# Queries and keys projected feature-major and stacked by DMA, and a new order of units at the attention's end

## Chip, cores and metric

The kernel runs on one core of one Trainium2 chip. The metric is device time in microseconds (us) of that core, from one launch that does the whole step. Nothing else runs on the core.

## What is computed

One step of a two-layer network for 128 context tokens and 512 latent tokens. Each layer has three branches that read one input projection: a state-space mixer, differential attention, and a gated MLP. The change lies in the attention branch. Cut to that branch, the reference is:

```python
q = q.reshape(bt, T, DA_HEADS, 2, DA_QK)            # 8 heads, 2 maps, 64 wide
k = k.reshape(bt, T, DA_HEADS, 2, DA_QK)
v = v.reshape(bt, T, DA_HEADS, DA_VD)               # 128 wide
if latent:                                          # 512 tokens; context: 128, no rotary
    k_all = concatenate([ctx_k, apply_rope(k, cos, sin)], 1)   # 128 cached keys first
    v_all = concatenate([ctx_v, v], 1)
    q = apply_rope(q, cos, sin)
s = einsum("bqhmd,bkhmd->bhmqk", q, k_all) * DA_QK ** -0.5
p = softmax(s, axis=-1)
w = p[:, :, 0] - lam * p[:, :, 1]
o = rmsnorm(einsum("bhqk,bkhd->bqhd", w, v_all), head_norm_w) * (1 - lam_init)
y_b = o.reshape(bt, T, DA_INNER) * silu(g_b)
```

`apply_rope` takes the 64 numbers of a map as two halves of 32 and returns `[x1*c - x2*s, x1*s + x2*c]`. Everything is float32 in the interface. To keep that precision, the kernel splits an operand into a rounded high part (type fp32r) and a low part that holds the rest, and sums the products of the parts that matter.

## The kernel before, in words

The 640 tokens are five tiles of 128; tile 0 is the context. The work is a list of units (`schedule`). A unit is one slice of a weight matrix, and each is computed as three products of parts (high x high, high x low, low x high) over eight blocks of 128 features:

- T units (`dense_T`, L469 to L471) hold a token tile in the array and stream weights: the result has tokens on the partitions. For each tile there are 24 matmuls, as wide as the unit.
- F units (`dense_F`, L529 to L531) hold weights and stream tokens: the result has features on the partitions and tokens along the row. There are two halves of 320 tokens, 24 matmuls each.

Per layer the order is eight T units qkvg (one a head: q, k, v and gate, 512 columns), three T units sv of the MLP (352 columns), then pairs of F units mgb and brb that gate and project the attention's output, and then the other branches (u, gc, xbc, mgc, brc, z, mga, bra) and the output projection wo.

Around this stream of dense matmuls run tasks. A task is a generator; it yields a number of ticks until its next step. A tick passes after three or six dense matmuls (`tick`), and it is the only clock: what a task issues is put into the engines' queues at that place in the order. `force` runs ticks without matmuls until a condition holds. `w_advance` loads weights (512 KB a chunk, L383 on SyncE's queue), copies the high part on ScalarE (L405) and subtracts the low part on VectorE (L414); up to five chunks stand ready. The list is run once with a stand-in for the engines, a plan places all buffers, and then it is run again to write the instructions.

For each head and tile, `head_evac` takes the projection out of PSUM with tokens on partitions, rotates q and k there (L849, L852, L853, on VectorE), splits both (`split_k`, `split_q`), transposes four blocks that hold the stacked high and low parts (L870) and one with q's low part (L871), and copies them out of PSUM (L876, L880). `head_cache` does the same for the cached keys with two transposes (L895). `scores` is one task for each head and tile: for each map the stacked high part of q against the stacked parts of k (L917, 128 rows high), and the low part of q against the high part of k (L922, 64 rows high, the two maps on the two halves of the array); row maxima (L929), exponentials with sums (L935), the combined weights (L942), their transposes (L951), and the product with v (L968). It uses two pairs of PSUM banks, of the group "s". `head_y` normalises, gates and transposes the head's output; `split_b` splits the eight outputs for the brb units. Scores of head h run while head h+1 is projected (`before`), those of head 7 beside the first sv unit.

## Time and profile before

| | |
|---|---|
| median of 3 runs | 2299.95 us (2299.92 to 2301.16) |
| profiled execution | 2299.74 us, span 2298.0 us |
| TensorE busy | 2253.0 us, 98% |
| VectorE busy | 1416.6 us, 62% |
| ScalarE busy | 1018.7 us, 44% |
| DMA | 218.52 MB, mean 95 GB/s |
| granted TensorE clock | 0.994 of full speed |

The page gives the busy time of each engine, the span in 40 slices, the chain of work that ended last, and the costliest groups of instructions. The start and length of a matmul row in the timeline are not its price: matmuls overlap, so the price of one in a stream is the distance from its start to the next one's. The attention stages lie at about 60 to 450 us (layer 0) and 1170 to 1600 us (layer 1) of the span.

### The profile page before, as it was taken

Reading aid. Unit: us, or ns where it says so; the run is one execution under the profiler, and the core shown is the slowest. Engines: PE = TensorE matmul, PEld = TensorE weight load, DVE = VectorE, ACT = ScalarE, POOL = GpSimd, SP = SyncE. Lnnn points to the kernel's source line nnn. Section 1 sums busy time; section 2 is a strip of 40 time slices with the busy share of each in tenths; the row PEclk is TensorE's granted clock in tenths of the full one; section 3 lists DMA queues with packets and bytes.
Section 4 is the critical chain, followed back from the end, with each engine's and each line's share of the span. In section 5 each row is a group of like instructions: output and inputs, shape, how many; then the busy total and the mean of one; then the engine's idle time right before and its main releaser. Section 6 shows DMA issues by size and latency. Waiting matters only on the chain.

```text
span 2298.0 us, 37200 instructions
## 1 busy us (share of the span) xinstructions
PE 2253.0 (98%) x14618; PEld 2044.9 (89%) x14618; DVE 1416.6 (62%) x2918; ACT 1018.7 (44%) x2386; POOL 184.8 (8%) x196
## 2 busy tenths in 40 slices
PE   7999999999999999999989999999999999999998
PEld 4788888999999999998868888889999999999986
DVE  6777777652454258976377777776424432789754
ACT  4555555521333247662265555554223322677421
POOL 1000000000100112320000000000000101132100
PEclk9999999999999999999999999999999999999999
DMA  7121110333223235534231112102222231555351
GB/s 287 56 63 43 60 59 29 107 131 129 92 65 104 83 82 147 164 104 158 90 115 64 43 60 63 61 18 98 83 74 74 66 112 57 143 138 147 105 184 46
DMA packets 80551, 218.52 MB, mean 95 GB/s; under 512 B 10284, under 2 KB 23660, under 8 KB 80376
## 3 DMA queue, kind: packets, MB, share of 16 engines
q1 hardware_dynamic: 80376, 216.15, 29.3%
q8 instruction: 115, 1.88, 0.4%
q14 instruction: 60, 0.49, 0.1%
HBM read 206.37 MB, written 8.68 MB: 94 GB/s over the span
## 4 chain that ended last, share of the span: by engine, by line
PE 84%; DVE 7%; ACT 4%; issue 2%; DMA 2%; SPq 0%; POOL 0%; DVEq 0%; ACTq 0%; POOLq 0%
PE psum L529 14%; PE psum L530 14%; PE psum L531 14%; PE psum L469 10%; PE psum L470 9%; PE psum L471 8%; PE psum L968 3%; PE psum L917 2%; PE psum L951 2%; PE psum L922 2%; PE psum L666 1%; DVE rounded L414 1%; PE psum L870 1%; PE psum L1088 1%; DMA plain<-csd 1%
## 5 line engine op out<-in xcount | busy, mean ns | idle before, releaser
L530 PE MATMUL psum<-shared,rounded 128*128 128x320 f32 x2624 | 812.2, 310 | 5.8 <-DVE shared L1062 5.8
L529 PE MATMUL psum<-shared,rounded 128*128 128x320 f32 x2624 | 816.5, 311 | 0.0
L531 PE MATMUL psum<-shared,rounded 128*128 128x320 f32 x2624 | 810.5, 309 | 0.0
L529 PEld LDWEIGHTS psum<-shared,rounded 128*128 128x128 f32 x2624 | 497.2, 189 | 19.0 <-issue 14.3
L530 PEld LDWEIGHTS psum<-shared,rounded 128*128 128x128 f32 x2624 | 492.9, 188 | 8.3 <-DVE shared L1062 7.3
L531 PEld LDWEIGHTS psum<-shared,rounded 128*128 128x128 f32 x2624 | 493.2, 188 | 0.0
L414 DVE TENSOR_TENSOR rounded<-plain,rounded 128x1024 fp32r<-128x1024 f32 (+2 forms) x214 | 266.0, 1244 | 250.0 <-ACT rounded L405 240.1
L469 PE MATMUL psum<-rounded,shared 128*128 128x512 f32 (+1 forms) x900 | 362.0, 402 | 2.1 <-DVE plain L1034 2.1
L470 PE MATMUL psum<-rounded,shared 128*128 128x512 f32 (+1 forms) x900 | 339.8, 378 | 0.0
L471 PE MATMUL psum<-rounded,shared 128*128 128x512 f32 (+1 forms) x900 | 338.7, 376 | 0.9 <-DVE shared L796 0.9
L405 ACT CAST rounded<-plain 128x1024 fp32r<-128x1024 f32 (+2 forms) x214 | 222.8, 1043 | 212.4 <-PE psum L530 194.1
L469 PEld LDWEIGHTS psum<-rounded,shared 128*128 128x128 f32 x900 | 170.0, 189 | 35.4 <-issue 10.3
L471 PEld LDWEIGHTS psum<-rounded,shared 128*128 128x128 f32 x900 | 169.8, 189 | 31.0 <-DVE shared L796 1.2
L470 PEld LDWEIGHTS psum<-rounded,shared 128*128 128x128 f32 x900 | 170.6, 190 | 20.8 <-DVE rounded L414 0.5
L1600 ACT ACTIVATE plain<-psum 128x320 f32<-128x320 f32 x96 | 41.6, 436 | 205.8 <-PE psum L531 198.4
L929 DVE TENSOR_REDUCE plain<-psum 128x1 f32<-128x640 f32 (+1 forms) x160 | 107.1, 711 | 35.8 <-PE psum L922 35.8
L935 ACT ACTIVATE plain<-psum,plain 128x640 f32<-128x640 f32 (+1 forms) x160 | 111.0, 699 | 21.0 <-DVE plain L929 17.4
L876 DVE CAST shared<-psum 128x512 fp32r<-128x512 f32 x64 | 44.2, 691 | 99.6 <-PE psum L870 99.4
L968 PEld LDWEIGHTS psum<-plain 128*128 128x128 f32 x640 | 81.0, 191 | 4.7
L974 ACT ACTIVATE plain<-psum,plain 128x128 f32<-128x128 f32 x80 | 29.4, 368 | 119.0 <-PE psum L968 103.2
L968 PE MATMUL psum<-plain 128*128 128x128 f32 x640 | 81.7, 275 | 0.0
L1028 ACT ACTIVATE plain<-psum 128x320 f32<-128x320 f32 (+1 forms) x62 | 27.8, 448 | 106.1 <-PE psum L531 69.4
(321 smaller groups left out, 3017.6 us busy)
## 6 DMA issues: line engine op xcount, KB each, us to landing
plain<-in_wp_dram SPq DMA_DIRECT2D x248, 512.0 KB
shared<-in_wp_dram SPq DMA_DIRECT2D x44, 512.0 KB
shared<-csd SPq DMA_DIRECT2D x33, 320.0 KB
plain<-csd SPq DMA_DIRECT2D x31, 320.0 KB
plain<-in_wp_dram SPq DMA_DIRECT2D x12, 528.0 KB
shared<-ecd SPq DMA_DIRECT2D x34, 128.0 KB
plain<-ecd SPq DMA_DIRECT2D x30, 128.0 KB
plain<-in_xin_dram SPq DMA_DIRECT2D x7, 512.0 KB
```

Source lines behind the costliest of these rows:

```text
L405: self.nc.scalar.copy(self.r(blk[0], 0, sz), self.v(self.w_raw[i], 0, sz))
L414: self.nc.vector.tensor_tensor(out=self.r(blk[1], 0, sz), in0=self.v(raw, 0, sz), in1=self.v(blk[0], 0, sz), op=ALU.subtract)
L469: mm(out, ht, wh, start=(k == 0), stop=False)
L470: mm(out, ht, wl, start=False, stop=False)
L471: mm(out, lt, wh, start=False, stop=(k == KD - 1))
L529: mm(out, wh, xh, start=(k == 0), stop=False)
L530: mm(out, wh, xl, start=False, stop=False)
L531: mm(out, wl, xh, start=False, stop=(k == KD - 1))
L917: mm(self.P[:, ss[m] + half, 0:n], q, k, start=True, stop=False)
L929: nc.vector.tensor_reduce(out=self.v(st, m, 1), in_=src[m], op=ALU.max, axis=AX.XY if t else AX.X, negate=True)
L935: nc.scalar.activation(pv, src[m], AF.Exp, bias=self.v(st, m, 1), accum_out=self.v(st, 2 + m, 1))
L968: mm(out, self.v(wt, 128 * j, 128), self.v(H["v"], 128 * j, 128), start=(j == 0), stop=(j == 4))
```

## The change

q and k leave the T unit. Each head has an F unit q and an F unit k of 128 features, whose result has features on the partitions and all 640 tokens along the row. v and the gate stay token-major, in T units vg of two heads (512 columns, heads 0 and 1) and then of one head (256 columns). The cached keys come from the host with features first, and the new keys leave so.

- `rope_evac` copies the halves out of PSUM into `raw`, swaps the 32-row halves of each map by four SBUF-to-SBUF transfers (`sw`), multiplies `raw` and `sw` by tables, and adds.
- For q it writes the scaled high part of map m into rows 64m to 64m+63 and the low part there into a second copy, and fills the other 64 rows by four transfers, so that one copy holds high over low and the other low over high. For k it stacks high and low with two transfers.
- `scores` then has, for each map and half, two matmuls of 128 rows. All four products of parts are in them. Its yield ahead of the product with v is longer by two ticks, and the one behind it by one.
- `split_k`, `split_q`, `head_evac` and `head_cache` are gone, with all their transposes.
- A head's five score tasks start from `rope_evac`, seven ticks apart, and for heads 6 and 7 four ticks apart.
- After the heads come all eight mgb units, then brb with the sv units between them. `split_b` takes each head as it is ready.
- The plain buffer grows and the rounded one shrinks by 1732 columns; the rotation tables are now 128 x 512 each.

```diff
-SIZE_F, SIZE_R, SIZE_X = 22140, 10180, 10240
+SIZE_F, SIZE_R, SIZE_X = 23872, 8448, 10240
...
-D_CACHE, D_SCORES, D_CACHE0, D_W0 = 5, 2, 4, 0
+D_SCORES, D_LAST, D_W0 = 7, (4, 4), 0
+D_SWAP = (1, 5, 6)
...
     for l in range(DEPTH):
+        u.append(("T", "vg", l, 0, 512))
         for h in range(8):
-            u.append(("T", "qkvg", l, h, 512))
-        for b in range(3):
-            u.append(("T", "sv", l, b, 352))
+            u.append(("F", "q", l, h, 128))
+            u.append(("F", "k", l, h, 128))
+            if h < 6:
+                u.append(("T", "vg", l, h + 2, 256))
+
+        mgb, brb = [("F", "mgb", l, d, 128) for d in range(8)], []
         for d in range(8):
-            u.append(("F", "mgb", l, d, 128))
-            u.append(("F", "brb", l, d, 128))
-            if l + 1 < DEPTH:
-                u.append(("M", d % 2, l + 1, d // 2, 512))
+            brb.append([("F", "brb", l, d, 128)] + ([("M", d % 2, l + 1, d // 2, 512)] if l + 1 < DEPTH else []))
+        sv = [("T", "sv", l, b, 352) for b in range(3)]
+        for x in (mgb, brb[0], brb[1], sv[:1], brb[2], sv[1:2], brb[3], sv[2:], *brb[4:]):
+            u += x
...
+    def vg_evac(self, heads, t, b):
...
+            nc.scalar.activation(self.v(th), self.P[:, b, 256 * i + 128:256 * i + 256], AF.Tanh, scale=0.5)
+            dst = self.v(H["v"], 128 * t, 128) if t else self.v(H["vc"])
+            nc.scalar.copy(dst, self.P[:, b, 256 * i:256 * i + 128])
...
+    def rope_evac(self, H, x, half, b):
...
+        n = 640 if x == "q" else 768
+        if half == 0:
+            H["raw" + x] = self.al(n)
+        raw = H["raw" + x]
+        nc.scalar.copy(self.v(raw, 320 * half, 320), self.P[:, b, 0:320])
+        self.give(b)
+        if half == 0:
+            if x == "k":
+                nc.sync.dma_start(out=self.v(raw, 640, 128), in_=a["cache_k"][l, h])
+            return
+        yield D_SWAP[0]
+        sw = self.al(512)
+        for p in range(0, 128, 32):
+            q = p ^ 32
+            nc.sync.dma_start(out=self.v(sw, 0, 512, p, p + 32), in_=self.v(raw, 128, 512, q, q + 32))
+        if x == "k":
+            nc.sync.dma_start(out=a["o_k"][l, h], in_=self.v(raw, 0, 128))
+        yield D_SWAP[1]
+        nc.vector.tensor_tensor(out=self.v(raw, 128, 512), in0=self.v(raw, 128, 512), in1=self.cc, op=ALU.mult)
+        nc.vector.tensor_tensor(out=self.v(sw), in0=self.v(sw), in1=self.ss, op=ALU.mult)
+        yield 1
+        nc.vector.tensor_tensor(out=self.v(raw, 128, 512), in0=self.v(raw, 128, 512), in1=self.v(sw), op=ALU.add)
...
+        if x == "q":
+            X = H["q"] = self.alr(4 * 640, True)
+            for m in range(2):
+                p = (64 * m, 64 * m + 64)
+                nc.scalar.activation(self.r(X, 640 * m, 640, *p), self.v(raw, 0, 640, *p), AF.Copy, scale=0.125)
+            yield 3
...
+            for m in range(2):
+                p, q = (64 * m, 64 * m + 64), (64 - 64 * m, 128 - 64 * m)
+                nc.sync.dma_start(out=self.v(X, 1280 + 640 * m, 640, *q), in_=self.v(X, 640 * m, 640, *p))
+                nc.sync.dma_start(out=self.v(X, 640 * m, 640, *q), in_=self.v(X, 1280 + 640 * m, 640, *p))
         else:
...
+                nc.sync.dma_start(out=self.v(K, 768 * m, 768, *q), in_=self.v(L, 0, 768, *p))
+            self.fr(L)
+        yield D_SWAP[2]
+        H["ok"].add(x)
+        if len(H["ok"]) == 2:
+            for t in range(NT):
+                self.go(self.scores(H, t), 1 + D_SCORES * t if h < 6 else 1 + D_LAST[1] * (h - 6) + D_LAST[0] * t)
+            self.go(self.head_y(H), D_LAST[0] * NT)
...
         for m in range(2):
-            q = self.r(H["qk"], (2 + m) * 640 + 128 * t, 128)
             for half in range(2 if t else 1):
-                k = self.r(H["qk"], m * 640 + 320 * half, 320) if t else self.r(H["kc"], 128 * m, 128)
-                mm(self.P[:, ss[m] + half, 0:n], q, k, start=True, stop=False)
-        for half in range(2 if t else 1):
-            for m in range(2):
-                r0, r1 = 64 * m, 64 * m + 64
-                k = self.r(H["qk"], m * 640 + 320 * half, 320, r0, r1) if t else self.r(H["kc"], 128 * m, 128, r0, r1)
-                mm(self.P[:, ss[m] + half, 0:n], self.r(H["ql"], 128 * t, 128, r0, r1), k, start=False, stop=True)
+                k = self.r(H["k"], 768 * m + (128 + 320 * half if t else 0), n)
+                for i in range(2):
+                    mm(self.P[:, ss[m] + half, 0:n], self.r(H["q"], 1280 * i + 640 * m + 128 * t, 128), k, start=(i == 0), stop=(i == 1))
...
         def split_b():
-            yield from self.until(lambda: not self.heads)
+            yield from self.until(lambda: "scored" in self.heads[7])
             self.yt = self.operand(8)
             for f in range(8):
+                yield from self.until(lambda: f in self.yb)
```

The order of the instructions shows this at three places. First TensorE, in the projection of a head in layer 0. Before, a tile's transposes (L870, L871) stand between dense matmuls (L469 to L471, 512 wide) and the products with v (L968):

```order
L968 MATMUL psum<-plain 128x128 x5
L469 MATMUL psum<-rounded,shared_65 128x512
L470 MATMUL psum<-rounded,shared_65 128x512
L471 MATMUL psum<-rounded,shared_65 128x512
L870 MATMUL psum<-rounded 128x128 x4
L871 MATMUL psum<-rounded 128x128
```

In the changed kernel a vg unit of 256 columns (its lines are L472 to L474) has the product with v (L956) and eight score matmuls (L909) in one place, and there are no other transposes than those of the softmax weights and of the head's output:

```order
L474 MATMUL psum<-rounded,shared_65 128x256
L956 MATMUL psum<-plain 128x128 x5
L909 MATMUL psum<-shared_398 128x320 x8
L472 MATMUL psum<-rounded,shared_65 128x256
L473 MATMUL psum<-rounded,shared_65 128x256
```

What moved: one row of five transposes of rounded parts is out of each tile, the dense rows are half as wide, and the score matmuls have become eight of one kind.

Second SyncE's queue, for one head. Before, L842 and L843 write the new keys and values, L825 and L826 read the cached ones, and the rest are weights (L383):

```order
L383 DMA plain<-in_wp_dram 128x1024 x3
L825 DMA plain<-in_cache_k_dram 128x128
L826 DMA plain<-in_cache_v_dram 128x128
L383 DMA plain<-in_wp_dram 128x1024
L842 DMA out_o_k_dram<-plain 128x128
L843 DMA out_o_v_dram<-plain 128x128
```

In the changed kernel, L847 are the swaps, L871 and L872 the stacking of q, L887 that of k, L849 and L817 write keys and values, and L388 are the weights:

```order
L847 DMA plain<-plain 32x512 x4
L849 DMA out_o_k_dram<-plain 128x128
L388 DMA plain<-in_wp_dram 128x1024
L817 DMA out_o_v_dram<-plain 128x128
L871 DMA shared_398<-shared_398 64x640
L872 DMA shared_398<-shared_398 64x640
L871 DMA shared_398<-shared_398 64x640
L872 DMA shared_398<-shared_398 64x640
L887 DMA shared_398<-shared_398 64x768 x2
L388 DMA plain<-in_wp_dram 128x1024 x2
```

What moved: fourteen transfers within SBUF for each head now stand in the same queue as the weights.

Third VectorE, where a tile (before) or a head's q (after) is rotated. Before, the rotation of one tile reads PSUM (L849, L852), and L876 copies transposes:

```order
L849 TENSOR_TENSOR plain<-psum,plain 128x256
L852 TENSOR_TENSOR plain<-psum,plain 128x256
L853 TENSOR_TENSOR plain<-plain 128x256
L855 SCALAR_TENSOR_TENSOR plain<-plain,psum 128x128
L954 COPY plain<-psum 128x128
L929 TENSOR_REDUCE plain<-psum 128x1 x2
L808 TENSOR_TENSOR rounded<-plain,rounded 128x128
L819 SCALAR_TENSOR_TENSOR rounded<-plain,rounded 128x128
L876 COPY shared_399<-psum 128x4x128
```

In the changed kernel, the rotation (L851, L852, L854) needs the swaps' landing, and score maxima (L917) and a weight's low half (L419) are behind it:

```order
L851 TENSOR_TENSOR plain<-plain 128x512
L852 TENSOR_TENSOR plain<-plain 128x512
L556 TENSOR_TENSOR plain<-plain 128x5
L917 TENSOR_REDUCE plain<-psum 128x1 x2
L854 TENSOR_TENSOR plain<-plain 128x512
L559 TENSOR_TENSOR plain<-plain 128x5
L562 SCALAR_TENSOR_TENSOR plain<-plain 128x5
L942 COPY plain<-psum 128x128
L419 TENSOR_TENSOR rounded<-plain,rounded 128x1024
```

What moved: a rotation of 512 columns, once for q and once for k, that waits for a transfer, in place of four rotations of 256 that wait for TensorE.

## Rows read from the trace of the kernel before

**Rows 1.** The page, part 1: engine, busy us, share of the span, instructions.
```profile
PE 2253.0 (98%) x14618; PEld 2044.9 (89%) x14618; DVE 1416.6 (62%) x2918; ACT 1018.7 (44%) x2386; POOL 184.8 (8%) x196
```
**Rows 2.** The page, part 4: the chain that ended last, by engine.
```profile
PE 84%; DVE 7%; ACT 4%; issue 2%; DMA 2%; SPq 0%; POOL 0%; DVEq 0%; ACTq 0%; POOLq 0%
```
**Rows 3.** Timeline, TensorE, 300 to 305 us: start us, length us, engine, line, operation.
```profile
300.40 0.28 PE L895 MATMUL psum<-rounded,shared 128*128 128x128 f32 x2
300.52 0.47 PE L469 MATMUL psum<-rounded,shared 128*128 128x512 f32 x1
300.83 0.40 PE L470 MATMUL psum<-rounded,shared 128*128 128x512 f32 x1
...
302.46 0.39 PE L471 MATMUL psum<-rounded,shared 128*128 128x512 f32 x1
...
304.30 0.46 PE L870 MATMUL psum<-rounded 128*128 128x128 f32 x4
304.59 0.25 PE L871 MATMUL psum<-rounded 128*128 128x128 f32 x1
304.68 0.46 PE L469 MATMUL psum<-rounded,shared 128*128 128x512 f32 x1
304.98 0.40 PE L470 MATMUL psum<-rounded,shared 128*128 128x512 f32 x1
```
**Rows 4.** Timeline, TensorE, 1000 to 1004 us, F units: first and last of 28.
```profile
1000.05 0.31 PE L530 MATMUL psum<-shared,rounded 128*128 128x320 f32 x1
...
1003.98 0.31 PE L530 MATMUL psum<-shared,rounded 128*128 128x320 f32 x1
```
**Rows 5.** Timeline, TensorE, 400 to 406 us, an sv unit: twelve dense matmuls, ten of L968.
```profile
400.12 0.32 PE L469 MATMUL psum<-rounded,shared 128*128 128x352 f32 x1
...
401.90 0.32 PE L471 MATMUL psum<-rounded,shared 128*128 128x352 f32 x1
402.06 1.28 PE L968 MATMUL psum<-plain 128*128 128x128 f32 x10
403.10 0.41 PE L469 MATMUL psum<-rounded,shared 128*128 128x352 f32 x1
403.34 0.32 PE L470 MATMUL psum<-rounded,shared 128*128 128x352 f32 x1
```
**Rows 6.** Timeline, TensorE, 1499.6 to 1502.2 us: one block of scores with transposes ahead.
```profile
1499.63 0.71 PE L951 MATMUL psum<-plain 128*128 128x128 f32 x5
1500.09 0.82 PE L917 MATMUL psum<-shared 128*128 128x320 f32 x4
1500.85 0.56 PE L922 MATMUL psum<-shared 64*128 64x320 f32 x4
1501.34 0.50 PE L469 MATMUL psum<-shared,shared 128*128 128x512 f32 x1
1501.67 0.40 PE L470 MATMUL psum<-shared,shared 128*128 128x512 f32 x1
```
**Rows 7.** Timeline, TensorE, 200 to 206 us: the scores of a context tile.
```profile
202.60 0.42 PE L917 MATMUL psum<-shared 128*128 128x128 f32 x2
202.95 0.33 PE L922 MATMUL psum<-shared 64*128 64x128 f32 x2
203.21 0.50 PE L469 MATMUL psum<-shared,shared 128*128 128x512 f32 x1
```
**Rows 8.** Timeline, SyncE, 725 to 737 us: four transfers of 64 partitions within SBUF.
```profile
730.16 2.47 SPq L1273 DMA_DIRECT2D plain<-plain  x4
```
**Rows 9.** The chain in order of time, 900 to 910 us: a transfer, start and length.
```profile
902.91 4.13 DMA shared<-csd
```
**Rows 10.** Groups by line and shape, whole span: count, busy us, mean ns, idle before.
```profile
L414 DVE TENSOR_TENSOR rounded<-plain,rounded 128x1024 fp32r<-128x1024 f32 x196 | 245.7, 1254 | 247.0 <-ACT rounded L405 237.1 <-DMA plain<-csd 5.9 <-DMA plain<-in_wp_dram 3.9
L929 DVE TENSOR_REDUCE plain<-psum 128x1 f32<-128x640 f32 x128 | 99.5, 819 | 35.8 <-PE psum L922 35.8
L853 DVE TENSOR_TENSOR plain<-plain 128x256 f32<-128x256 f32 x64 | 27.2, 426 | 2.2
L935 ACT ACTIVATE plain<-psum,plain 128x640 f32<-128x640 f32 x128 | 99.8, 785 | 19.6 <-DVE plain L929 15.9 <-DVE rounded L414 3.6
```

More of the change, by code (lines that the diff above doesn't have):

```diff
@@ L458, in dense_T @@
             b = self.take_d()
-            if before:
-                before(t)
             out = self.P[:, b, 0:n]
@@ L906, in scores @@
         mm = nc.tensor.matmul
-        yield from self.until(lambda: H["T"] >= ({0, 1, 2, 3, 4, "c"} if t else {0}))
         st = self.al(8)
@@ L967, in scores @@
             for j in range(5):
-                mm(out, self.v(wt, 128 * j, 128), self.v(H["v"], 128 * j, 128), start=(j == 0), stop=(j == 4))
+                mm(out, self.v(wt, 128 * j, 128), self.v(H["v"], 128 * ((j + 1) % 5), 128), start=(j == 0), stop=(j == 4))
         else:
@@ L1534, in layer @@
         self.group[6] = "t"
-        def before(h):
-            def f(t):
-                if h in self.heads:
-                    self.go(self.scores(self.heads[h], t), D_SCORES)
-            return f
-        for h in range(8):
-            def begin():
-                self.heads[h] = self.head_begin(l, h)
-            def evac_h(t, b):
-                return self.head_evac(self.heads[h], t, b)
-            if l + h:
-                begin()
-            if l + h > 1:
-                self.max_w = 5 if h < 7 else 4
-            if l + h:
-                self.dense_T(ui, self.h, evac_h, before(h - 1))
-            else:
-                self.dense_first(ui, self.h, evac_h, begin)
-            ui += 1
-        self.vln = [self.al(1024) for _ in range(NT)]
-        self.dt = self.al(160)
-        bn = self.al(5 * 12 + 10 + 10)
         def evac_sv(blk, t, b):
+            bn = state["bn"]
             n = 352 if blk < 2 else 320
@@ L1579, in layer, with begin, evac @@
         self.dtok = False
-        self.dense_T(ui, self.h, lambda t, b: evac_sv(0, t, b), before(7))
-        self.dense_T(ui + 1, self.h, lambda t, b: evac_sv(1, t, b))
         self.yt = None
         def split_b():
-            yield from self.until(lambda: not self.heads)
+            yield from self.until(lambda: "scored" in self.heads[7])
             self.yt = self.operand(8)
             for f in range(8):
+                yield from self.until(lambda: f in self.yb)
+                if f == 7:
+                    self.group[6] = "d"
                 yield from self.split_y(self.yt, f, self.yb.pop(f))
                 yield 2
+        while self.units[ui][1] in ("vg", "q", "k"):
+            kind, name, l_, h, n = self.units[ui]
+            if name == "vg":
+                hs = []
+                def begin(h=h, n=n, hs=hs):
+                    for i in range(h, h + n // 256):
+                        self.heads[i] = self.head_begin(l, i)
+                        hs.append(self.heads[i])
+                def evac(t, b, hs=hs):
+                    return self.vg_evac(hs, t, b)
+                if l == 0 and h == 0:
+                    self.dense_first(ui, self.h, evac, begin)
+                else:
+                    begin()
+                    self.dense_T(ui, self.h, evac)
+            else:
+                self.dense_F(ui, self.h, lambda half, b, H=self.heads[h], x=name: self.rope_evac(H, x, half, b))
+            ui += 1
         self.go(split_b())
-        self.dense_T(ui + 2, self.h, lambda t, b: evac_sv(2, t, b))
-        ui += 3
-        self.group[6] = "d"
         self.merged = {}
@@ L1612, in run_unit @@
                 self.mod_unit(ui)
+            elif name == "sv":
+                if i == 0:
+                    self.vln = [self.al(1024) for _ in range(NT)]
+                    self.dt = self.al(160)
+                    state["bn"] = self.al(5 * 12 + 10 + 10)
+                self.dense_T(ui, self.h, lambda t, b: evac_sv(i, t, b))
             elif name[:2] == "mg":
@@ L1751, in _pack @@
             m = w_mod[l][:, mod_cols(i)]
-        elif name == "qkvg":
-            m = np.concatenate([wi[:, o + 128 * i:o + 128 * i + 128] for o in (OFF_Q, OFF_K, OFF_V, OFF_GB)], 1)
+        elif name == "vg":
+            m = np.concatenate([wi[:, o + 128 * h:o + 128 * h + 128] for h in range(i, i + n // 256) for o in (OFF_V, OFF_GB)], 1)
         elif name == "sv":
```

170 lines of the change are left out of this document (59 added, 111 removed).

## Prediction

> **What bounds the kernel now.** I read the page first. TensorE is busy for 98% of the span and VectorE for 62% [rows 1], and the chain that ended last runs 84% over TensorE [rows 2]. A busy TensorE is modelled from matmuls that overlap, so I took prices from the timeline, as distances from one start to the next. In the attention stage the 512-column projection matmuls start 0.2329 us apart (302.46 less 300.83, seven steps) [rows 3]; the 320-column ones of the later stages 0.1456 us (1003.98 less 1000.05, 27 steps) [rows 4]; the 352-column ones 0.1618 us (401.90 less 400.12, 11 steps) [rows 5]. That is 0.455, 0.455 and 0.460 ns a column: dense matmuls of these widths are paid by the column, with no idle time between them. So time is won by taking work out of TensorE's stream, and lost where TensorE must wait.
>
> **The change part by part.** The sum is made against the profiled execution, 2299.74 us (span 2298.0 us), which is 0.2 us under the median of the three runs, 2299.95 us.
>
> *Transposes out.* head_evac turns five 128x128 blocks of each token tile (L870, L871). One such piece: from 304.30 to the next dense matmul at 304.68 is 0.38 us, and behind that one the next starts after 0.30 us instead of 0.233, 0.07 more: 0.45 us [rows 3]. Two layers of eight heads and five tiles make 80 pieces, -36.0 us. The cached keys' two transposes (L895) take 0.12 us, and the pair behind them 0.31 instead of 0.233: 0.20 us [rows 3], 16 times, -3.1 us. Nothing on TensorE takes their place: feature-major rows come out of the projection, and the stacking is done by DMA.
>
> *Projection.* Per layer 960 matmuls of 512 columns become 120 of 512, 720 of 256 (units vg) and 768 of 320 (units q and k): the same columns in all. Over both layers that is 1920 x 0.2329 = 447.2 us now, and 240 x 0.2329 + 1536 x 0.1456 + 1440 x p after. The trace has no dense 256-column matmul. By the column p is 0.116 to 0.118 us; I take 0.117, since three widths agree, which gives 448.0 us: +1 us. The far end is the price of the 128-column score matmuls below; it is rival B.
>
> *Scores.* For a tile of latents, from five transposes at 1499.63 over eight score matmuls to the dense matmul at 1501.34 is 1.71 us, and the dense pair behind takes 0.33 instead of 0.233: 1.81 us [rows 6]. Plain transposes and plain matmuls are paid 0.11 us an instruction: ten of L968 take 1.04 us, and 0.08 in the pair behind [rows 5]. So the five are 0.55 us and the eight 1.26 us. After the change these are eight full-height matmuls, 8 x 0.1456 = 1.17 us: -0.09 us, 64 times, -6 us, with bounds of -6 and 0. The same row shows the four half-height matmuls of L922 within 0.56 us. The Trainium skill (TensorEngine Tiling (Array Packing), section Key Properties) says that tiles on different rows of the array work in parallel, and that a change of the mode drains TensorE. By its first half alone this part would be rival D; the row's 1.26 us for eight agree with both halves together, pairs that run side by side and a switch that gives it back.
>
> For the context tile two 128-column matmuls and a half-height pair take 0.61 us [rows 7], some 0.20 us a pass; four full ones take 0.7 to 0.8 us: +1.5 us for 16 heads.
>
> TensorE's stream in sum: -36.0 - 3.1 + 1 - 6 + 1.5 = **-43 us**.
>
> *Waits that come.* After each q or k unit SyncE issues four transfers of 32 partitions, and VectorE's rotation stands six ticks behind the copy that they read (a tick is six dense matmuls: 0.87 us in q, k and mgb units, 0.70 us in vg), some 5 us. Four transfers took SyncE 2.47 us to issue [rows 8], and a transfer on the chain landed after 4.13 us with others in the queue [rows 9]: together 6.6 us, so VectorE can stand for up to 2 us, 32 times. Queued behind it are the weights' low halves (L414, 1.25 us each), for which the dense matmuls wait, and the score maxima (L929, 0.82 us each) [rows 10]. The weights are split two or three units ahead, 7 us each (48 x 0.1456), and the next score block is seven ticks away, so most of this is covered. VectorE is also relieved: per head it loses the copies of the transposes and twelve 256-wide rotations of 0.426 us [rows 10], against six of 512. I take +3 us; the bounds are 0 and 32 x 2 = +64.
>
> At the attention's end the scores of heads 6 and 7 come every four ticks beside mgb units. One round of the two score banks is 1.17 us of scores, two maxima (0.82 each) and two exponentials (0.785 each, with their sums' reads about 2.0 in all) [rows 10], with hops 5.4 us; four ticks with the attention's other pieces last 4 x 0.87 + 1.17 + 1.7 = 6.4 us. One us is spare, and other work takes some of it: +6 us for 20 blocks. The kernel before runs the same round beside its sv units: -5 us.
>
> Ahead of unit brb 0 the code runs 16 ticks with no matmul in them. They are places in an order, not time: the last head's small VectorE steps need nothing of TensorE, and TensorE needs the last slice only after 21 matmuls of brb, 3.1 us later. +1 us a layer, bounds 0 and 6.
>
> Sum: -43 + 3 + 6 - 5 + 2 = -37 us, **2263 us**.
>
> **The rivals.**
> *A. The swaps reach TensorE.* If VectorE stands long and its cover is thin, each of the 32 costs 0.75 us: +24 us, some 2284 us. From 1.2 us each (37 / 32) the whole gain is gone. For it: queues that keep their order, and 512 KB weight loads between the swaps on SyncE. Against: the seven-tick spacing.
> *B. 256 columns are too narrow.* A 128-column matmul of the context scores costs 0.20 us, 1.6 ns a column against 0.455 [rows 4, 7]. If 256 columns fall on that side, p is about 0.40 us, and 1440 x 0.283 = +408 us: 2670 us, slower than before. It decides from p = 0.143 on (37 / 1440 above 0.117). Against: from 512 down to 320 columns nothing rises.
> *C. A floor per matmul.* If spacing does not fall below the 0.146 us of 320 columns, 1440 x 0.029 = +41 us: 2304 us, no change. Against: the plain matmuls of 128 columns, with weights as large, pass at 0.11 us [rows 5].
> *D. The half-height pairs were worth two slots.* If each pair passed in the time of one matmul, giving the pairs up costs two slots in each of 64 blocks, 2 x 0.1456 x 64 = +19 us in place of -6: 2288 us. Against: the block's 1.26 us [rows 6], where six slots would be 0.87. (That is the tiles of the Trainium skill, named above, taken without the drain.)
>
> **How the numbers follow.** Forecast (2263 us, 2252 to 2276) 0.60; a gain without new waits (about 2250 us) 0.03; A 0.20, of which 0.03 is past the whole gain; B 0.09; C 0.06, of which 0.05 lies within 0.2%; D 0.02. Within 0.2% is 4.6 us, about what a measurement of this kernel can tell from no change. Faster: 0.60 + 0.03 + 0.17 + 0.02 = 0.82. Same: 0.05. Slower: 0.03 + 0.09 + 0.01 = 0.13. The range leaves out B, C and the worst of A, 0.18 in all: 2246 to 2292 us; its low end is the stream's -43 us with ten more from waits that go.
>
> **What would show it.** The lines of the transposes are gone, 432 instructions, and 1296 dense ones come for them. Starts of 256-column matmuls 0.117 us apart settle B and C; eight score matmuls in 1.17 us settle D. VectorE idle ahead of the rotation's first instruction, ended by a DMA, is A; it counts only where dense matmuls or score blocks of the attention stage are idle until VectorE releases them. If the stages behind (u, gc, xbc, z, wo) move by more than a few us, my accounting by stage is wrong.

## The result, and the profile after

The changed kernel takes 2239.7 us (median of 4 runs, 2235.34 to 2240.48) against 2300.16 us: a ratio of 0.9732, 95% interval 0.9716 to 0.9749. The gain is 60.5 us where 37 were forecast, and the time lies below the range, 2246 to 2292. The profiled execution is the one of 2239.7 us, with a span of 2237.7 us.

The page of the kernel after, parts 1 and 4, answers to [rows 1, 2]:

```profile
PE 2195.2 (98%) x15482; PEld 2106.5 (94%) x15482; DVE 1371.5 (61%) x2597; ACT 1022.2 (46%) x2242; POOL 186.0 (8%) x196
...
PE 84%; DVE 8%; ACT 4%; issue 2%; DMA 2%; SPq 0%; DVEq 0%; ACTq 0%
```

TensorE has 864 instructions more, which is 1296 dense ones come and 432 transposes gone, and still sets the end.

Where the time went is read at lines that both kernels have. These are the first and last starts of the MLP's mixing matmuls (L1088 before, L1078 after) and of L698, which runs beside the bra units; first the kernel before, then the kernel after:

```profile
L1088 PE MATMUL psum<-plain x160: 271/275/276, 601.1 to 1833.9; 128*128 128x128 f32 x160
L698 PE MATMUL psum<-plain x16: 591/592/593, 1084.3 to 2233.4; 128*128 128x512 f32 x16
```

```profile
L1078 PE MATMUL psum<-plain x160: 270/275/275, 575.1 to 1777.5; 128*128 128x128 f32 x160
L698 PE MATMUL psum<-plain x16: 592/593/593, 1056.2 to 2173.7; 128*128 128x512 f32 x16
```

In layer 0, 26.0 us are won up to the mixing matmuls (601.1 less 575.1), and 2.1 more behind them. In layer 1 it is 59.7 by L698, of which 3.3 fall between the last mixing matmul and there (1833.9 less 1777.5 is 56.4). The attention brings most, but stages whose code is the same have moved too.

The prices of the new matmuls, from the timeline of TensorE: 20 steps of 256 columns, then eight scores of a latent tile, then the scores of a context tile behind their transposes.

```profile
214.01 0.28 PE L472 MATMUL psum<-rounded,shared 128*128 128x256 f32 x1
...
216.36 0.28 PE L474 MATMUL psum<-rounded,shared 128*128 128x256 f32 x1
```

```profile
208.71 1.33 PE L909 MATMUL psum<-shared 128*128 128x320 f32 x8
209.88 0.28 PE L472 MATMUL psum<-rounded,shared 128*128 128x256 f32 x1
...
176.96 0.64 PE L909 MATMUL psum<-shared 128*128 128x128 f32 x4
177.44 0.36 PE L532 MATMUL psum<-shared,rounded 128*128 128x320 f32 x1
```

256 columns cost 0.1175 us (2.35 / 20), eight scores 1.17 us, four context scores 0.48 us.

In the attention stage TensorE has one wait of more than 1 us in all that it did not have before. By the waits of the kernel after, a vg unit's first matmul in a PSUM bank waits for L821, the product of VectorE that empties the bank. The timeline of VectorE, and TensorE's row at the end, show one of these waits:

```profile
PE psum L472 <- DVE plain L821: 5.8, 8, 1.2
```

```profile
245.22 0.28 DVE L821 SCALAR_TENSOR_TENSOR plain<-plain,psum 128x128 f32<-128x128 f32 x1
245.42 0.61 DVE L982 SCALAR_TENSOR_TENSOR plain<-plain 128x128 f32<-128x128 f32 x2
245.95 1.55 DVE L917 TENSOR_REDUCE plain<-psum 128x1 f32<-128x640 f32 x2
247.41 0.68 DVE L851 TENSOR_TENSOR plain<-plain 128x512 f32<-128x512 f32 x1
248.01 0.68 DVE L852 TENSOR_TENSOR plain<-plain 128x512 f32<-128x512 f32 x1
248.73 0.69 DVE L854 TENSOR_TENSOR plain<-plain 128x512 f32<-128x512 f32 x1
249.34 0.28 DVE L942 COPY plain<-psum 128x128 f32<-128x128 f32 x1
249.54 0.28 DVE L821 SCALAR_TENSOR_TENSOR plain<-plain,psum 128x128 f32<-128x128 f32 x1
...
249.87 0.39 PE L472 MATMUL psum<-rounded,shared 128*128 128x256 f32 x1 [1.23 <-DVE plain L821]
```

Between two L821 VectorE is never free: maxima, rotation and a copy stand in front. In starts, the eight waits are 7.0 us over the usual spacing.

### The profile page after: what moved, and what is told of

It is laid out like the page before. It is cut to its first block, busy times and chain, and to the rows that moved or that the text cites. A ratio compares the mean times of both kernels' runs of the same rounds, so it can differ in the third digit from the quotient of the medians.

```text
span 2237.7 us, 38780 instructions
## 1 busy us (share of the span) xinstructions
PE 2195.2 (98%) x15482; PEld 2106.5 (94%) x15482; DVE 1371.5 (61%) x2597; ACT 1022.2 (46%) x2242; POOL 186.0 (8%) x196
## 4 chain that ended last, share of the span: by engine, by line
PE 84%; DVE 8%; ACT 4%; issue 2%; DMA 2%; SPq 0%; DVEq 0%; ACTq 0%
PE psum L533 19%; PE psum L534 18%; PE psum L532 18%; PE psum L472 5%; PE psum L473 5%; PE psum L474 5%; PE psum L909 3%; PE psum L956 3%; PE psum L939 1%; PE psum L666 1%; PE psum L1078 1%; ACT plain L923 1%; ACT rounded L410 1%; PE psum L1335 1%; DMA plain<-csd 1%
## 5 line engine op out<-in xcount | busy, mean ns | idle before, releaser
L533 PE MATMUL psum<-shared,rounded 128*128 128x320 f32 x3136 | 972.1, 310 | 4.7 <-DVE shared L1052 4.7
L532 PE MATMUL psum<-shared,rounded 128*128 128x320 f32 x3136 | 973.5, 310 | 0.4 <-DVE plain L1024 0.4
L534 PE MATMUL psum<-shared,rounded 128*128 128x320 f32 x3136 | 965.0, 308 | 0.0
L532 PEld LDWEIGHTS psum<-shared,rounded 128*128 128x128 f32 x3136 | 591.6, 189 | 17.8 <-issue 13.5
L533 PEld LDWEIGHTS psum<-shared,rounded 128*128 128x128 f32 x3136 | 589.8, 188 | 7.2 <-DVE shared L1052 6.1
L534 PEld LDWEIGHTS psum<-shared,rounded 128*128 128x128 f32 x3136 | 591.4, 189 | 0.0
L419 DVE TENSOR_TENSOR rounded<-plain,rounded 128x1024 fp32r<-128x1024 f32 (+2 forms) x226 | 280.1, 1240 | 201.7 <-ACT rounded L410 197.1
L410 ACT CAST rounded<-plain 128x1024 fp32r<-128x1024 f32 (+2 forms) x226 | 235.7, 1045 | 204.3 <-PE psum L533 192.3
L472 PE MATMUL psum<-rounded,shared 128*128 128x256 f32 (+2 forms) x920 | 297.9, 324 | 5.8 <-DVE plain L821 5.8
L473 PE MATMUL psum<-rounded,shared 128*128 128x256 f32 (+2 forms) x920 | 291.7, 317 | 0.2 <-DVE rounded L419 0.2
L474 PE MATMUL psum<-rounded,shared 128*128 128x256 f32 (+2 forms) x920 | 290.9, 316 | 0.9 <-DVE shared L796 0.9
L472 PEld LDWEIGHTS psum<-rounded,shared 128*128 128x128 f32 x920 | 173.4, 188 | 18.7 <-DVE plain L821 7.4
L474 PEld LDWEIGHTS psum<-rounded,shared 128*128 128x128 f32 x920 | 173.5, 189 | 10.6 <-DVE shared L796 1.5
L473 PEld LDWEIGHTS psum<-rounded,shared 128*128 128x128 f32 x920 | 173.4, 188 | 9.5 <-DVE rounded L419 0.9
L917 DVE TENSOR_REDUCE plain<-psum 128x1 f32<-128x640 f32 (+1 forms) x160 | 107.7, 713 | 87.2 <-PE psum L909 86.1
L909 PE MATMUL psum<-shared 128*128 128x320 f32 (+1 forms) x576 | 99.8, 312 | 0.0
L909 PEld LDWEIGHTS psum<-shared 128*128 128x128 f32 x576 | 84.6, 189 | 0.7 <-ACT plain L923 0.4
L956 PE MATMUL psum<-plain 128*128 128x128 f32 x640 | 81.3, 274 | 0.0
```

The lines of the kernel that those rows point to most:

```text
L410: self.nc.scalar.copy(self.r(blk[0], 0, sz), self.v(self.w_raw[i], 0, sz))
L419: self.nc.vector.tensor_tensor(out=self.r(blk[1], 0, sz), in0=self.v(raw, 0, sz), in1=self.v(blk[0], 0, sz), op=ALU.subtract)
L472: mm(out, ht, wh, start=(k == 0), stop=False)
L473: mm(out, ht, wl, start=False, stop=False)
L474: mm(out, lt, wh, start=False, stop=(k == KD - 1))
L532: mm(out, wh, xh, start=(k == 0), stop=False)
```

## The experiments

Each was timed beside the kernel before. The ratio is to that kernel, with its 95% interval.

### The unit order alone

The kernel before with the order of the change.

```
-            u.append(("T", "sv", l, b, 352))
...
+        for x in (mgb, brb[0], brb[1], sv[:1], brb[2], sv[1:2], brb[3], sv[2:], *brb[4:]):
+            u += x
...
+            self.go(self.scores(self.heads[7], t), 3 + 4 * t)
```

> The kernel before with one part of the change alone: the order of units at the attention's end (eight mgb units, two brb, then the sv units one by one between brb units; the last head's scores every four ticks). Projection, transposes and scores stay. New account, read from the two traces: beside its sv units the kernel before loses 8.6 us in both layers (four score blocks that cost 2.71 us where the others cost 1.83, four waits of 0.7 us ahead of 352-column matmuls, 1.9 us at the transposes of the softmax), and these go with nothing new: 2291 us (2288 to 2294). The prediction's account (-5 for the old loop, +6 for the new one, +2 ahead of brb 0): 2303 us. A rival, that the order is worth nothing: 2300 us.

2294.3 us, 0.9977 (0.9968 to 0.9987): -6 us, just outside the first account's range, and clear of the second account and of no change. The forecast of +3 for this part had the wrong sign. The waits of TensorE on a PSUM bank that VectorE's gelu product frees, four ahead of sv units in the kernel before, and the only one here:

```profile
PE psum L469 <- DVE plain L1034: 2.1, 4, 0.6
```

```profile
PE psum L528 <- DVE plain L1033: 0.4, 1, 0.4
```

The one that is left is ahead of an F unit at 1715.6 us, so the sv units have none. In the new order sv runs when a third bank has been given to the dense units and the scores are over; which of the two takes the waits away was not tested.

### The transposes, and the delay of the softmax chain

The transposes of q, k and the cached keys are left out, and their copies read the rows that were not turned:

```
-            nc.tensor.transpose(self.PR[:, b0, 128 * j:128 * j + 128], self.r(qd, 128 * j, 128), self.identr)
-        nc.tensor.transpose(self.PR[:, b1, 0:128], self.r(qd, 512, 128), self.identr)
...
-        src = self.PR[:, b0, :].rearrange("p (b n) -> p b n", b=4)
+        src = self.r(qd, 0, 512).rearrange("p (b n) -> p b n", b=4)
```

> The kernel before without the transposes of q, k and the cached keys: what copied the transposed block out of PSUM copies the block as it was from SBUF, so VectorE and ScalarE have the same instructions, and the scores are computed from rows that were not turned. The prediction's account: 80 x 0.45 + 16 x 0.20 = 39.1 us: 2261 us. New account from the trace of before, every such block with its waits: 38.4 + 6.5 = 45 us, less up to 3 us where the wait of the first cached keys of layer 1 moves to the next piece: 2256 us (2254 to 2259). Rival: the gain of the changed kernel (60 us) is the transposes with more that hangs on them (bank turnover, TensorE's mode): 2245 us or less.

2273.7 us, 0.9888 (0.9873 to 0.9902): -26 us. All three accounts missed. TensorE's stream did get shorter by the forecast's 39 us: added up from start to start, 33.1 us of transposes are gone, and the dense steps take 6.4 us less. What is given back is idle time. The waits of TensorE ahead of the softmax's transposes (us in all, times, longest), in the kernel before (L951) and here (L946):

```profile
PE psum L951 <- ACT plain L974: 1.0, 2, 0.5
```

```profile
PE psum L946 <- DVE plain L937: 6.4, 15, 0.5
PE psum L946 <- ACT plain L845: 5.0, 12, 0.4
PE psum L946 <- ACT plain L969: 1.0, 2, 0.5
```

That is 12.4 us against 1.0. The stream in front became shorter, and TensorE came to the softmax's transposes before the combined weights that they read were done (L937, on VectorE behind ScalarE's exponentials). The rows that name ScalarE's L845 mean the same wait, as one of them shows (VectorE, ScalarE and the weight load; other rows left out):

```profile
193.81 0.88 DVE L937 SCALAR_TENSOR_TENSOR plain<-plain 128x640 f32<-128x640 f32 x1
...
194.53 0.27 ACT L845 COPY plain<-psum 128x128 f32<-128x128 f32 x1
...
194.81 0.42 PEld L946 LDWEIGHTS psum<-plain 128*128 128x128 f32 x4 [0.82 <-ACT plain L845]
```

L845 copies v, which the transposes do not read, and the weight load starts 0.12 us after L937 ends in 27 of 28 such waits, whether the row names L845 or not. The run also makes the copies on VectorE cheaper (0.42 us each from SBUF, 0.69 from PSUM), so it gives VectorE more room than the removal alone.

The next two runs move the softmax's transposes two ticks back, without and with the transposes of q and k. This delay is not in the change, which lengthens the two behind it:

```
         w = Pm[0]
-        yield 2
+        yield 4
```

> The run without the transposes of q, k and the cached keys, and with one delay more: the transposes of the softmax weights stand two ticks later behind the product that they read (4 ticks in place of 2). The run without the transposes alone gave back some 18 us: its trace has two waits of 0.57 us a head ahead of the softmax's transposes (for VectorE's product and a copy of ScalarE), +12 us, and +4 us at the start of layer 1. If the pacing of that chain is what ate the gain, most of the 12 us comes back: 2262 us (2259 to 2265). If the wait only moves to the next reader (the matmuls with V, or the score banks): 2270 to 2274 us.

2258.6 us, 0.9822 (0.9807 to 0.9836): the first account, and a little more. The waits ahead of L946 are gone.

> The kernel before with one delay more: the transposes of the softmax weights stand two ticks later behind their product. With the transposes of q and k gone the same delay gave 15 us. If those waits are there only because the stream ahead of them got shorter, this run gains what its own trace shows of them, about 3 us (0.17 us in each of 12 blocks of the context tile, and less elsewhere): 2297 us. If the delay is worth as much in the kernel before: 2285 us. If it only moves the wait to the next reader: 2300 us or more.

2317.9 us, 1.0077 (1.0059 to 1.0094): slower by 17.5 us. Only the third account, 2300 us or more, allowed for that, and it named no size. The four runs make a table:

| | delay 2 | delay 4 |
|---|---|---|
| with the transposes of q and k | 2300.2 | 2317.9 |
| without | 2273.7 | 2258.6 |

The same delay costs 17.5 us with them and brings 15 without. With them, they wait themselves. TensorE's largest wait ahead of L870 in this run (in the kernel before it is 0.2 us), and one such wait (VectorE, ScalarE and the weight load; other rows left out):

```profile
PE psum L870 <- ACT plain L935: 7.4, 11, 0.7
```

```profile
178.19 0.59 ACT L953 COPY plain<-psum 128x512 f32<-128x512 f32 x1 [1.92 <-DVE plain L556]
...
178.40 1.40 DVE L992 SCALAR_TENSOR_TENSOR plain<-plain 128x128 f32<-128x128 f32 x5
...
179.73 0.28 DVE L954 COPY plain<-psum 128x128 f32<-128x128 f32 x1
179.93 0.28 DVE L808 TENSOR_TENSOR rounded<-plain,rounded 128x128 fp32r<-128x128 f32 x1
...
180.13 0.21 ACT L935 ACTIVATION_READ_ACCUMULATOR plain<-psum,plain 128x1 f32 x1
180.32 0.40 PEld L870 LDWEIGHTS psum<-rounded 128*128 128x128 f32 x4 [1.09 <-ACT plain L935]
```

The row names ScalarE's L935, but the weight load starts before L935 ends, and ScalarE's copy out of the banks that both kinds of transposes share (L953) was long done. It starts 0.12 us after VectorE's L808, the low part of k, which L870 reads, and this distance is the same in all 13 long waits. With the delay, the second copy of the softmax's transposes (L954) stands right ahead of L808 in VectorE's queue, and in 12 of the 13 both stand behind the five products that end a head (L992). These waits are 8.7 us of the 17.5 (7.4, and 1.3 that name L808); 3.8 more are at the sv units (L469 behind L1034, 5.9 us against 2.1).

So in this kernel the transposes are worth 26 us at delay 2, 59 us at delay 4, and 42 us from the one to the other. The price of the piece, 0.45 us, says only what TensorE spends on them.

### The start of the weights' tile

The change sets two tile sizes anew, SIZE_F and SIZE_R. The tile of the rounded weights, behind the first, therefore starts at byte 95,488 and not at 88,560 of a partition's row, counted from the first tile. One run gives the kernel before a start that is a multiple of 64 (88,576), the other takes it from the changed kernel (95,440). That is 16 past a multiple of 64, and not 48, as the old start is and the expectation says. With either size the plan puts all blocks at the same offsets of their tiles (2073 in the kernel before, 1860 in the changed one), so nothing but the start moves:

```
-SIZE_F, SIZE_R, SIZE_X = 22140, 10180, 10240
+SIZE_F, SIZE_R, SIZE_X = 22144, 10176, 10240
...
-SIZE_F, SIZE_R, SIZE_X = 23872, 8448, 10240
+SIZE_F, SIZE_R, SIZE_X = 23860, 8460, 10240
```

> The kernel before with the two sizes of its SBUF tiles moved by four columns, so that the tile of the rounded weights starts at a multiple of 64 bytes (88,576 instead of 88,560); nothing else. The traces show 145.6 to 145.7 ns between 320-column matmuls in the three kernels with the old sizes and 144.8 in the five with the new ones, in stages whose code is the same. If the start of that tile is the cause, the price falls to 144.8 ns and the time by 7,900 x 0.8 ns, 6 to 7 us: 2293 us. If the cause is something else: 2300 us and 145.6 ns.

> The changed kernel with the tile of the rounded weights moved by 12 columns, to a start that is 48 bytes past a multiple of 64, as the kernel before has it. If the start of that tile is the cause of the cheaper 320-column matmuls, they cost 145.6 to 145.7 ns again and the time rises by 9,400 x 0.8 ns, 7 to 8 us: 2247 us. If not: 2239 to 2240 us and 144.8 ns.

The first: 2292.2 us, 0.9961 (0.9946 to 0.9976), -8 us, as the first account has it. The second: 2240.2 us, 0.9736 (0.9722 to 0.9751), no change in time, where 2247 was expected. The timeline of TensorE has a run of 749 matmuls of 320 columns, the same code in all kernels; its first and last start, for the kernel before, before with the new start, after, and after with its start moved:

```profile
738.76 0.31 PE L530 MATMUL psum<-shared,rounded 128*128 128x320 f32 x1
...
847.63 0.31 PE L531 MATMUL psum<-shared,rounded 128*128 128x320 f32 x1
```

```profile
737.39 0.31 PE L530 MATMUL psum<-shared,rounded 128*128 128x320 f32 x1
...
845.48 0.31 PE L531 MATMUL psum<-shared,rounded 128*128 128x320 f32 x1
```

```profile
712.18 0.31 PE L533 MATMUL psum<-shared,rounded 128*128 128x320 f32 x1
...
820.26 0.31 PE L534 MATMUL psum<-shared,rounded 128*128 128x320 f32 x1
```

```profile
711.45 0.31 PE L533 MATMUL psum<-shared,rounded 128*128 128x320 f32 x1
...
820.33 0.31 PE L534 MATMUL psum<-shared,rounded 128*128 128x320 f32 x1
```

Over 748 steps that is 145.5, 144.5, 144.5 and 145.6 ns: the start of the tile sets the price, in both directions. In the kernel before it holds for nearly all F units. In the changed kernel the price in the attention stage lies at 145.4 to 145.7 ns with either start, so only the later stages can lose: 0.75 ns in each of some 5,900 steps, 4 us. From the first mixing matmul of each layer on they take 1.8 us longer in this profile, the attention stages 1.7 us less, and the medians differ by 0.45 us, within the spread of the runs. So what the start is worth in time is shown for the kernel before; for the changed one only the price is.

### The form of the scores

The changed kernel with the low part as half-height pairs, first for the context tile, then for the latent tiles:

```
+                    p = (64 * m, 64 * m + 64)
+                    k = self.r(H["k"], 768 * m + (128 + 320 * half if t else 0), n, *p)
+                    mm(self.P[:, ss[m] + half, 0:n], self.r(H["q"], 1280 + 640 * m + 128 * t, 128, *p), k, start=False, stop=True)
```

> The changed kernel with the context tile's scores as the kernel before has them: two 128-row matmuls and two of 64 rows in place of four of 128 rows (the low part of the sum is cut to 64 rows of the stacked tile). The prediction's account: the pair form is cheaper by 0.09 us, 16 times: 2238 us. New account: 0.79 us a block with pairs behind the softmax's transposes against 0.45 us without, 16 times 0.34: 2245 us.

2240.0 us, 0.9743 (0.9728 to 0.9757): no change. By the timeline the block with pairs takes 0.61 us up to the next dense matmul (as in [rows 7]) where four full ones take 0.48:

```profile
175.48 0.42 PE L909 MATMUL psum<-shared 128*128 128x128 f32 x2
175.83 0.33 PE L914 MATMUL psum<-shared 64*128 64x128 f32 x2
176.09 0.41 PE L532 MATMUL psum<-shared,rounded 128*128 128x320 f32 x1
```

That would be 2 us in 16 blocks, and not the 0.34 a block that I expected.

> The changed kernel with the latent tiles' scores as the kernel before has them: four 128-row matmuls of 320 columns and four of 64 rows in place of eight of 128 rows (the low part of the sum is cut to 64 rows of the stacked tile), the context tile unchanged. New account: 1.284 us for the eight in before against 1.168 in after, 64 times 0.116: 2247 us. The prediction's account 0.09 x 64: 2246 us. Rival D, that half-height pairs pass two in the time of one: 64 x 2 x 0.146 less: 2221 us.

2245.4 us, 0.9764 (0.9748 to 0.978): +6 us. The block, to be set beside 208.71 to 209.88 above:

```profile
208.46 0.75 PE L909 MATMUL psum<-shared 128*128 128x320 f32 x4
209.14 0.56 PE L914 MATMUL psum<-shared 64*128 64x320 f32 x4
209.63 0.39 PE L472 MATMUL psum<-rounded,shared 128*128 128x256 f32 x1
209.85 0.28 PE L473 MATMUL psum<-rounded,shared 128*128 128x256 f32 x1
```

1.17 us for eight here too. The first dense step behind takes 0.22 us (209.85 less 209.63) instead of 0.11. Inside the block, the four of 64 rows take 0.49 us where four of 128 rows take 0.58, but the four ahead of them take 0.68: the change from 128 to 64 rows costs what the pairs save. Rival D is out. The Trainium skill (TensorEngine Tiling (Array Packing), section Key Properties) has both halves of this: tiles that work in parallel, and a change of mode that drains TensorE. The rows agree with the two together.

### The swaps

```
-            nc.sync.dma_start(out=self.v(sw, 0, 512, p, p + 32), in_=self.v(raw, 128, 512, q, q + 32))
```

The rotation multiplies the rows of the copy itself.

> The changed kernel without the swap transfers (four a q or k unit, 128 in all): the rotation multiplies the copy's own rows, so its VectorE work is the same and waits for no transfer; q and k are rotated with the wrong halves. Rival A of the prediction in full (0.75 us for each of 32 swaps reach TensorE): 24 us faster, 2216 us. The prediction's sum (+3 us for the swaps): 2237 us. New account: TensorE waits for no swap in the trace, 2239 to 2240 us, no change.

2238.2 us, 0.9731 (0.9715 to 0.9746): 1.5 us less, within the spread of the runs. In the kernel after, VectorE waits for a swap three times in 32:

```profile
DVE plain L851 <- DMA plain<-plain: 5.8, 3, 3.5
```

No row of TensorE's waits comes from it. Rival A is out.

### The new wait of the vg units

First, the five products that end a head stand six ticks later, so that they leave the crowd ahead of L821:

```
+        yield 6
         for t in range(NT):
...
-        yield 7
+        yield 3
```

> The changed kernel with one delay moved: the five products that end a head on VectorE (L982) stand six ticks later, their transposes at most two ticks later. The trace of after shows eight waits of a vg tile's first matmul for VectorE's L821, 5.8 us in all, with the products (1.6 us), the rotation (2.0 us), two maxima (1.6 us) and the split of q (1.7 us) ahead of L821 in VectorE's queue. If that queue is the cause, most of these waits go: 2234 us (2232 to 2236). If the waits come from something else (ScalarE's tanh, the swap transfer): 2239 to 2240 us.

2240.6 us, 0.9741 (0.9728 to 0.9753): no gain. Eight waits of 0.4 to 1.4 us became 18 shorter ones, with 8.0 us in all: the products had moved ahead of the next tile's L821. So this does not tell the queue from another cause. Second, ScalarE copies the gate out of PSUM and frees the bank:

```
+            nc.scalar.copy(self.v(H["g"], 128 * t, 128), self.P[:, b, 256 * i + 128:256 * i + 256])
...
+        self.give(b)
+        yield 2
```

> The changed kernel with the gate half of a vg tile copied out of PSUM by ScalarE, which then frees the bank; VectorE's product (L821) reads the copy two ticks later. After's trace has eight waits of a vg tile's first matmul for L821, 0.4 to 1.4 us, 7.0 us of excess in all; a later place of the products of a head only spread them (18 waits, 8.0 us). If VectorE's queue holds the bank, the waits are gone: 2233 us (2231 to 2236). If ScalarE's longer queue (80 times two copies of 0.28 us) takes its place: 2238 to 2242 us.

2230.3 us (2229.41 to 2233.53), 0.9696 (0.968 to 0.9712): 9.4 us under the changed kernel, and below both. Ahead of L472, what ended idle time in the kernel after, and then here:

```profile
  DVE plain L821: 13.1, 16
  DVE plain L1104: 2.5, 3
```

```profile
  DVE plain L1105: 2.5, 3
```

The cause of these waits was a bank that VectorE held, with its queue in front of the one instruction that would free it. The waits account for 7.0 of the 9.4 us; the rest is not traced.

### The parts together, and the chain's other delays

Four parts at once in the kernel before: no transposes of q and k, the delay of the softmax's transposes, the order, the start of the tile. The delay is not a part of the change.

> The kernel before with four parts at once: no transposes of q, k and the cached keys (the scores then come from rows that were not turned), the softmax's transposes two ticks later, the unit order of the changed kernel at the attention's end, and the tile of the rounded weights on a multiple of 64 bytes. Alone against the kernel before they gave -42 (the first two together), -6 and -8.4 us. If the parts add: 2300 - 56 = 2244 us. If the waits that are left without the transposes (5 us of them ahead of the 352-column matmuls of sv, 2.6 us twice) go with the order: 2239 us. If the order and the delay take away the same waits: 2249 us or more. Full-height scores (-6 us by the run with pairs put back) are the one part of the gain that it lacks.

2241.0 us, 0.9745 (0.9728 to 0.9761): -59 us where the single ones add to -56. That it comes near the change's 60.5 shows no shares: it has a delay that the change lacks, and lacks the new projection, the new scores and the wait at L821. The last run takes the two delays that the change does lengthen back to what they were:

```
         self.fr(w)
-        yield 4
+        yield 2
         b = yield from self.take("t")
...
         self.fr(wt)
-        yield 2
+        yield 1
```

> The changed kernel with two delays of the score chain as the kernel before has them: the matmuls with V stand two ticks behind the copies of the softmax's transposes (4 in the change), and their evacuation one tick later (2 in the change). These delays are a part of the change that the prediction did not price. If they are what brings the last 6 us that the single parts leave unexplained, the time rises to 2246 us, with TensorE idle ahead of L956 until ScalarE or VectorE releases it. If they bring nothing: 2239 to 2240 us, and those 6 us stay open.

2261.8 us, 0.9839 (0.9822 to 0.9855): +22 us, far more than either theory. TensorE's longest waits in this run; the kernel after has none at these two lines:

```profile
PE psum L956 <- ACT plain L991: 14.5, 10, 2.1
PE psum L988 <- DVE plain L942: 11.1, 8, 1.4
```

The matmuls with V and the transposes of a head's output now wait for copies that empty the banks they share and are still in ScalarE's and VectorE's queues. The waits at L821 go in exchange, so 22 us are the net.

## Why the prediction was wrong

The sign, the engine that bounds and the prices held; the sum was too small by 23.5 us. Where it failed is read from the two timelines of TensorE, added up from each start to the next, less the idle time that the profile marks. The attention stages end at a layer's first mixing matmul, and the later ones at its last L698 (in layer 1 at the end). The forecasts of transposes and scores hold the dense step behind them, which these rows count as dense. What the table leaves out of the attention stages is 114.7 us before and 114.6 after.

| us | before | after | change | forecast |
|---|---|---|---|---|
| transposes of q, k and cached keys | 33.1 | 0 | -33.1 | -39.1 |
| dense matmuls of the attention stages, without sv | 802.2 | 791.8 | -10.4 | +1 |
| scores | 90.4 | 86.8 | -3.6 | -4.5 |
| the softmax's transposes | 32.5 | 30.0 | -2.5 | none |
| sv | 120.3 | 115.9 | -4.4 | -5 |
| idle time in the attention stages | 19.8 | 20.3 | +0.5 | +11 |
| later stages | 1067.5 | 1061.1 | -6.4 | 0 |

The first step that failed, and the largest, is "waits that come": +11 us (swaps 3, the loop of heads 6 and 7 6, ahead of brb 0 2) of which the rows show none; the idle time rose by 0.5 us, with 5.8 us at L821 in it that the sum did not have. The second is the later stages, put at nothing: -6.4 us. The third is the stream, -43 us against -49.6 (the first four rows): some 4 us of it are the context tile's scores (9.8 to 7.5 us by the rows, forecast +1.5), 2.5 the softmax's transposes. Point by point:

- **Prices in the stream: right.** 256 columns at 0.1175 (forecast 0.117), which ends rivals B and C. Eight scores in 1.17 us, -6 us by the run with pairs put back (forecast -6). The projection cost some +2 us by the spacings (forecast +1).
- **The context tile's scores: wrong sign, small.** I priced full-height passes at 0.18 to 0.20 us from a row that mixes them with a half-height pair [rows 7]. Plain matmuls of that width stand at 0.11 us in [rows 5], and four full ones came to 0.48 us: 0 to -2 us instead of +1.5.
- **The transposes: sized right, and counted in full without a reason.** The run without them shows that the 39 us leave the stream, and that 12 can come back as idle time at the softmax's transposes: a shorter stream reaches the softmax chain sooner. I priced new waits only at the swaps, the last two heads and brb 0. In the changed kernel the chain gives nothing back (0.9 us at L939, none at L956), so the count in full came true; but I had not looked at what feeds that chain, so this was luck.
- **The delays in the score chain: left out.** They stand in the change as 2 to 4 and 1 to 2, and I gave them no term. With the old ones the changed kernel is 22 us slower, at 2261.8 us. They do not explain why the sum was too small, since the sum had no wait there either; they are what made that true. That the run with the old delays lands on the forecast of 2263 us is chance.
- **The order at the end: forecast +3 (-5 + 6 + 2), measured -6.** The waits beside sv were worth about what I said (-4.4 us by the rows, forecast -5). The loop of heads 6 and 7 was to cost 6 us. That loop was a sum of busy times with a guess on top, and the kernel after has two waits there, 0.9 us together, at L939.
- **The swaps: +3 forecast, none found,** nor any in the forced ticks ahead of brb 0, where TensorE's waits name none.
- **The later stages: forecast unmoved, moved by 2.1 and 4.3 us** from the first mixing matmul of a layer on. That was my own test of the accounting, and it points to a line that I read as bookkeeping. The start of the weights' tile alone takes some 5 us off these stages in the kernel before, and 1.8 in the changed one, so a part of the 6.4 stays open.
- **The vg banks: +7 us, not forecast.** I named what is queued behind the rotation on VectorE as weights and maxima, and missed L821, which holds one of two dense banks. It took back part of the gain.

The rows say where the time went, not what each part of the change would bring alone: in the kernel before, the same removal is worth 26 or 59 us as the delay behind it stands. What is shown of the delays in the change is that without them a third of the gain is gone.

## What to carry to other kernels

When work is taken out of the engine that bounds, do not count it as won until the chain that feeds the next piece has been given room. Try the removal with one more and one less of each delay behind it, since the same delay can cost with the work in place and pay without it. A bank of the bounding engine should not wait for an instruction with other work queued ahead of it; here a copy on another engine freed it at once and won 9.4 us. A changed buffer size may be a change of speed until a timeline of the same code shows the same spacing. And where the profile names what ended a wait, check that the waiting instruction reads it, and that the distance from its end is the same each time.

## What was not expected of the hardware

A tile of stationary weights that starts 48 bytes past a multiple of 64 made a 320-column matmul 1.05 ns dearer (145.55 against 144.50 ns over 748 steps), and so did a start 16 bytes past one (145.56 against 144.50), each in a kernel whose other start is a multiple of 64. All these starts are multiples of 16 bytes. No other remainders were tried, and why the changed kernel's attention stage stays at 145.4 to 145.7 ns with either start is open.
